# A hybrid block on one Trainium2 core: begun blocks stored from ScalarE's queue, and a fourth sum made on the way up

## The chip, the core and the metric

The kernel runs on one core of one Trainium2 chip. A core has five engines with instruction queues of their own: PE (TensorE, matrix products into the eight banks of PSUM), DVE (VectorE), ACT (ScalarE), POOL (GpSimd) and SP (SyncE, which here issues the transfers). Each engine takes its instructions in the order of its queue and waits on semaphores for the others. A transfer (DMA) is issued by an engine's queue and then runs on 16 DMA engines that all queues share. The metric is device time in microseconds (us), lower is better.

## What is computed

One layer over 1024 tokens of width 1024, in float32: three mixers side by side (mLSTM, stick-breaking attention, an S5 state space), an output projection, and then a gated feed-forward network (FFN). The change is in the FFN alone:

```python
h = rmsnorm(x, norm_ffn_g[l])
up = h @ ffn_w_up[l]                      # 1024 x (2 * 2816)
g, v = up[..., :D_FF], up[..., D_FF:]
g = causal_dwconv(g, ffn_conv_w[l])       # 3 taps along the tokens
x = x + (jax.nn.silu(g) * v) @ ffn_w_down[l]
```

## The kernel before

Values are split in two parts, high and low, and each product is made of three (high by high, high by low, low by high). Both matrix products of the FFN run by a Strassen-Winograd scheme: a 2 by 2 partition of the matrices with seven products instead of eight, in which sums of the quarters are multiplied.

On the way up, the 2816 hidden features are 22 blocks `f` of 128. `others` makes the sums of a block's weights on DVE (`ss`), and `split` casts each to its high part on ACT (`wh`) and subtracts for the low part on DVE (`wl`). `up` makes the products, twelve matmuls of 128x512 each (`product`), into banks `pw`, `pv` and `pz`: `b11`, `t2`, `b21`, `t1`, `t3`, `t4`, `b22`. DVE and ACT take them out: `u2 = pv + p1` and `u3` are partial sums, `tv` is the value half and `pad` (`gs` in the profile) the gate half, to which the convolution (`cv`, with a Silu on ACT) is applied, and `tv` becomes the gated result.

The products `b11` and `b21` need only the unsplit input's first half, so ten blocks (`NPRE`) are begun before the other sums are ready: `keep` makes these two products, `put` copies each from PSUM into a tile `p1` on ACT and stores it in device memory (`kept`). `up` of such a block loads them back, the first into a `p1` tile (`L646`, `p<-kept`), the second into the gate half (`L647`, `gs<-kept`). The `p1` tiles come from four buffers. `order` lets a begun block and one that wasn't begun follow each other; two such blocks are a pair.

At the end of each pair `up` makes the sums that the product on the way down needs from the two gated results `one` and `tv` (`L682` to `L687`): it stores `tv`, then `one` with its second half replaced by a difference, then `ts`. These are `bd[at, 0..2]`. On the way down `fetch` loads halves of them (`tr`), `tokens` splits them (`th`, `tl`), and for the operand `t4` it loads two and subtracts one from the other. Seven products over the eleven pairs follow.

The order of the instructions on each engine is set by the tile framework's scheduler from the order of the code, priorities and its own timeline; buffers of a pool are given out by tags. So the same lines may stand elsewhere in the queues when other lines are added. All transfers are on SP's queue.

Of the kernel before, what the change touches and what calls it, by code (L numbers as in the profile page):

```python
# [10 lines left out]
F32 = mybir.dt.float32  # L11
# [9 lines left out]
P = 128  # L21
# [13 lines left out]
HT = T // 2  # L35
# [45 lines left out]
class Kernel:  # L81
# [467 lines left out]
    def ffn(self):  # L549


        nc, a = self.nc, self.a
# [6 lines left out]
        NPAIR = NF // 2  # L559
        order = [f for x in zip(range(NPRE - 1), range(NPRE, 2 * NPRE - 1)) for f in x] + list(range(2 * NPRE - 1, NF)) + [NPRE - 1]  # L560
        bd = {(at, i): self.dram.tile([P, T], F32, name=f"bd{at}_{i}") for at in range(NPAIR) for i in range(3)}
        t1, t2 = slice(0, HT), slice(HT, T)

        def parts(x, tag):
# [28 lines left out]
        def product(ps, w, b, more=False):  # L593

            n = 0
            for k in range(4):
                (rh, rl), lh, ll = B[b][k], *(x[:, k * P:(k + 1) * P] for x in w)
                for l, r in ((lh, rh), (lh, rl), (ll, rh)):
                    nc.tensor.matmul(out=ps, lhsT=l, rhs=r, start=n == 0 and not more, stop=n == 11, skip_group_check=more)  # L599
                    n += 1  # L600


        kept = {f: self.dram.tile([2, P, HT], F32, name=f"kept{f}") for f in range(NPRE)}
# [9 lines left out]
        def put(f, i):  # L613
            pw = begun[f][0]
            s = half_tile("p1", 4)
            nc.scalar.copy(out=s, in_=pw)
            nc.sync.dma_start(out=kept[f][i - 1], in_=s)

        keep(0, 1)
        self.last_scale(bank("s"))  # L620
        st_fa, fa = self.pool("ffa", side="left", waits="tile")
        half_tile = lambda n, c: fa.tile([P, HT], F32, tag=n, name=n, bufs=c)
        put(0, 1)
        for f in range(NPRE):
            if f + 1 < NPRE:
                keep(f + 1, 1)
                put(f + 1, 1)
            keep(f, 2)
            put(f, 2)
# [11 lines left out]
        def up(f, w):  # L641
            pad = gs[f % 2]
            tv = fb.tile([P, T], F32, tag="tv", name="tv", bufs=3)
            p1, u2, u3 = half_tile("p1", 4), fb.tile([P, HT], F32, tag="u2", name="u2"), fb.tile([P, HT], F32, tag="u3", name="u3")
            if f in kept:
                nc.sync.dma_start(out=p1, in_=kept[f][0])  # L646
                nc.sync.dma_start(out=pad[:, 2:2 + HT], in_=kept[f][1])  # L647
            else:
                pw = bank("w")
                product(pw, w[1], "b11")  # L650
                nc.scalar.copy(out=p1, in_=pw)
            pv = bank("v")
            product(pv, w[6], "t2")
            self.add(u2, pv, p1)
            if f not in kept:
                product(pw, w[2], "b21", True)
                nc.scalar.copy(out=pad[:, 2:2 + HT], in_=pw)
            pz = bank("z")
            product(pz, w[5], "t1")
            pv = bank("v")  # L660
            product(pv, w[7], "t3")
            self.add(u3, pv, u2)
            self.add(tv[:, t2], pz, u3)
            pv = bank("v")
            product(pv, w[4], "t4")
            self.add(tv[:, t1], pv, u3)
            product(pz, w[3], "b22", True)
            self.add(pad[:, 2 + HT:2 + T], pz, u2)
            c = fb.tile([P, T], F32, tag="cv", name="cv", bufs=2)
            self.act(c, pad[:, 0:T], AF.Copy, scale=cw[:, f, 0:1])  # L670
            for i in range(1, 3):
                self.stt(c, pad[:, i:i + T], cw[:, f, i:i + 1], c, ALU.mult, ALU.add)
            self.act(c, c, AF.Silu)
            self.mul(tv, c, tv)
            at, second = divmod(order.index(f), 2)
            if not second:
                self.first = tv
                return

            one = self.first  # L680
            nc.sync.dma_start(out=bd[at, 0], in_=tv)
            ts = fb.tile([P, T], F32, tag="ts", name="ts")  # L682
            self.sub(ts[:, t1], tv[:, t2], one[:, t2])
            self.sub(one[:, t2], one[:, t2], one[:, t1])
            self.sub(ts[:, t2], tv[:, t2], one[:, t2])
            nc.sync.dma_start(out=bd[at, 1], in_=one)
            nc.sync.dma_start(out=bd[at, 2], in_=ts)  # L687

        def block(r, c, k):

            tag = ("wv", "wt")[k % 2]
            raw = wq.tile([P, 512], F32, tag=tag, name=tag, bufs=2)
            nc.sync.dma_start(out=raw, in_=a["w_dn"][order[2 * k + c]][:, r * 512:r * 512 + 512])
            return raw

        for f, after in zip(order, order[1:] + [None]):
            this = ws
            if after is not None:
                ws = others(after, *gate_row(after, after not in kept))
            else:  # L700
                early = [block(0, 0, k) for k in range(4)]
                early = [(raw, parts(raw, "wx")) for raw in early]
            up(f, this)
# [9 lines left out]
        operand = {"b21": (0, t1), "b22": (0, t2), "b11": (1, t1), "t1": (1, t2), "t3": (2, t1), "t2": (2, t2)}  # L713
# [3 lines left out]
        x = {}  # L717

        def fetch(n, k):
            at, cols = operand[n]  # L720
            r = dt.tile([P, HT], F32, tag="tr", name="tr", bufs=4)
            nc.sync.dma_start(out=r, in_=bd[k, at][:, cols])
            return r

        def tokens(n, k):
            r = fetch("b21" if n == "t4" else n, k)
            if n == "t4":
                self.sub(r, r, fetch("t2", k))
            w = tuple(dt.tile([P, HT], F32R, tag=t, name=t, bufs=6) for t in ("th", "tl"))
            self.split(w, r)  # L730
            return w
# [83 lines left out]
        for p, n in ((1, "b11"), (2, "b21"), (7, "t3"), (6, "t2"), (4, "t4"), (5, "t1"), (3, "b22")):  # L815
            chained, last = p in (2, 3), p == 3
            if not chained:
                ps = [bank("d") for _ in range(4)]
            ends = []
            for k in range(NPAIR):  # L820
                w, b = weights(p, k), tokens(n, k)
                if last and k >= NPAIR - 5:
                    ends.append((k, w, b))
                else:
                    for m in range(4):
                        accumulate(ps[m], k, m, w, b, chained)
                between(p, k)
            for m in range(4):
                for k, w, b in ends:
                    accumulate(ps[m], k, m, w, b, chained)  # L830
                for cols in (slice(0, 256), slice(256, 512)) if last and m == 3 else (t1,):
                    with self.tc.high_priority():
                        evict(p, m, ps[m][:, cols], cols)
# [819 lines left out]
```

## Time and profile before

| | us |
|---|---|
| median of 3 runs | 1221.27 (1219.47 to 1224.64) |
| the profiled execution's own time | 1223.04 |
| its span in the trace | 1221.3 |
| PE, DVE, ACT, POOL busy in the span | 1188.3, 968.1, 632.9, 107.2 |

The mean granted clock of TensorE is 0.997 of full speed. The span has four stretches here: all that lies ahead of the FFN, to 580.3 us; the begun blocks and the sums of the input, to 643.8; the way up, to some 1008.5; the way down, to 1217.5. Matmuls are pipelined, and a modelled duration of 0.39 us stands on each of 128x512, while they start 0.227 us apart. An engine's line in a timeline says when an instruction started, how long it took, and in brackets how long the engine had been idle and what the profile takes for the releaser.

### The profile page before, as it was taken

The numbers are of one execution on the slowest core, as the hardware profiler recorded it, in microseconds if no ns is written. First come the engines' busy times: TensorE is split into PE (matmuls) and PEld (weight loads), VectorE is DVE, ScalarE is ACT, GpSimd is POOL, SyncE is SP. The second block draws the span as 40 slices with busy tenths as digits, with TensorE's granted clock in tenths as the row PEclk, the third lists the DMA queues.
The fourth block names the chain that finished last, engine by engine and source line by source line (L and its number), as shares of the span: only waits on it lengthen the run. The fifth ranks groups of instructions, "written<-read, shape, count | busy, mean of one in ns | idle before, by whom it ended". The sixth has DMA issues, their size and how long they took to land.

```text
span 1221.3 us, 17857 instructions
## 1 busy us (share of the span) xinstructions
PE 1188.3 (97%) x6543; PEld 1020.1 (84%) x6543; DVE 968.1 (79%) x1645; ACT 632.9 (52%) x1106; POOL 107.2 (9%) x100
## 2 busy tenths in 40 slices
PE   7899999999999999999999999999999999999998
PEld 6898999988899897787778888888888887888787
DVE  7898988899876588757886888888888676787874
ACT  6433588878786634444653333333344346664441
POOL 0000110201004655100000000000000000000000
PEclk9999999999999999999999999999999999999999
DMA  6431420101104201375372434443333257884563
GB/s 230 145 64 43 104 70 1 35 18 54 42 27 115 61 8 53 110 232 167 124 253 80 133 134 138 137 127 107 121 121 97 94 176 258 267 276 145 161 206 115
DMA packets 78855, 148.15 MB, mean 121 GB/s; under 512 B 10376, under 2 KB 16144, under 8 KB 78768
## 3 DMA queue, kind: packets, MB, share of 16 engines
q1 hardware_dynamic: 78768, 147.02, 38.1%
q8 instruction: 51, 0.84, 0.3%
q14 instruction: 36, 0.29, 0.1%
HBM read 110.21 MB, written 36.18 MB: 120 GB/s over the span
## 4 chain that ended last, share of the span: by engine, by line
PE 65%; DVE 17%; issue 7%; DMA 6%; ACT 4%; SPq 1%; POOL 0%; DVEq 0%; POOLq 0%; ACTq 0%
PE pv L599 15%; PE pd L812 12%; PE pj L156 11%; PE pz L599 10%; PE pw L599 10%; DVE sl L1174 4%; DMA tr<-bd 2%; PE first L156 2%; DVE cacc L113 1%; DVE srl L97 1%; ACT sl L121 1%; DVE zn L97 1%; DMA qk<-qkd 1%; DVE srl L110 1%; ACT srl L121 1%
## 5 line engine op out<-in xcount | busy, mean ns | idle before, releaser
L516 ACT CAST wh<-ss 128x512 fp32r<-128x512 f32 x88 | 53.6, 618 | 128.1 <-PE pz L599 81.2
L812 PE MATMUL pd<-tl,wh 128*128 128x512 f32 x292 | 114.0, 390 | 2.0 <-DVE tl L97 2.0
L156 PE MATMUL pj<-wh,hh 128*128 128x256 f32 x384 | 111.5, 290 | 1.5 <-ACT sg L121 1.2
L812 PE MATMUL pd<-th,wh 128*128 128x512 f32 x292 | 111.3, 390 | 1.0 <-ACT th L516 1.0
L812 PE MATMUL pd<-th,wl 128*128 128x512 f32 x292 | 112.0, 389 | 0.0
L156 PE MATMUL pj<-wh,hl 128*128 128x256 f32 x384 | 109.7, 286 | 0.0
L156 PE MATMUL pj<-wl,hh 128*128 128x256 f32 x384 | 108.9, 284 | 0.0
L1174 DVE TENSOR_TENSOR_SCAN sl<-sl,srl 128x256 f32<-128x256 f32 (+3 forms) x90 | 75.5, 871 | 22.9 <-ACT sl L121 22.3
L156 PEld LDWEIGHTS pj<-wh,hh 128*128 128x128 f32 x384 | 73.3, 191 | 3.5 <-ACT sg L121 1.6
L156 PEld LDWEIGHTS pj<-wl,hh 128*128 128x128 f32 x384 | 73.3, 191 | 0.9 <-issue 0.2
L156 PEld LDWEIGHTS pj<-wh,hl 128*128 128x128 f32 x384 | 73.3, 191 | 0.4 <-issue 0.4
L516 ACT CAST th<-tr 128x512 fp32r<-128x512 f32 x77 | 47.3, 618 | 42.2 <-DVE tr L97 25.4
L121 ACT ACTIVATE sl<-sl 128x512 f32<-128x512 f32 x108 | 68.0, 630 | 1.4
L812 PEld LDWEIGHTS pd<-tl,wh 128*128 128x128 f32 x292 | 54.8, 188 | 14.5 <-DVE tl L97 3.1
L812 PEld LDWEIGHTS pd<-th,wh 128*128 128x128 f32 x292 | 54.7, 188 | 12.8 <-ACT th L516 1.4
L97 DVE TENSOR_TENSOR wl<-ss,wh 128x512 fp32r<-128x512 f32 x88 | 60.2, 686 | 5.7 <-ACT wh L516 4.5
L812 PEld LDWEIGHTS pd<-th,wl 128*128 128x128 f32 x292 | 54.8, 188 | 11.2
L97 POOL TENSOR_TENSOR wl<-wr,wh 128x512 fp32r<-128x512 f32 x28 | 38.3, 1368 | 286.3 <-DVE wh L142 203.2
L113 DVE SCALAR_TENSOR_TENSOR cv<-gs,prm,cv 128x1024 f32<-128x1024 f32 x44 | 56.4, 1281 | 3.9 <-ACT cv L121 3.8
L97 DVE TENSOR_TENSOR tl<-tr,th 128x512 fp32r<-128x512 f32 x77 | 52.3, 685 | 7.4 <-ACT th L516 7.4
L1200 PEld LDWEIGHTS pv<-sbv,saT 128*128 128x128 f32 x432 | 53.9, 192 | 1.8
L1200 PE MATMUL pv<-sbv,saT 128*128 128x64 f32 x432 | 53.4, 269 | 0.0
(480 smaller groups left out, 3414.1 us busy)
## 6 DMA issues: line engine op xcount, KB each, us to landing
tr<-bd SPq DMA_DIRECT2D x88, 256.0 KB, 3.3
wt<-w_up SPq DMA_DIRECT2D x44, 256.0 KB, 2.7
bd<-tv SPq DMA_DIRECT2D x22, 512.0 KB, 2.9
wv<-w_up SPq DMA_DIRECT2D x32, 256.0 KB, 3.0
wr<-w_up SPq DMA_DIRECT2D x32, 256.0 KB, 3.2
wv<-w_dn SPq DMA_DIRECT2D x30, 256.0 KB, 3.5
wr<-w_out SPq DMA_DIRECT2D x28, 256.0 KB, 3.3
wt<-w_dn SPq DMA_DIRECT2D x25, 256.0 KB, 4.0
```

The lines of the kernel that those rows point to most:

```text
L97: (eng or self.nc.vector).tensor_tensor(out=out, in0=a, in1=b, op=op)
L110: (eng or self.nc.vector).tensor_scalar(out=out, in0=a, scalar1=s1, scalar2=s2, op0=op0, **kw)
L113: self.nc.vector.scalar_tensor_tensor(out=out, in0=a, scalar=s, in1=b, op0=op0, op1=op1)
L121: self.nc.scalar.activation(out=out, in_=a, func=f, **kw)
L156: self.nc.tensor.matmul(out=ps, lhsT=l, rhs=r, start=n == 0, stop=n == last)
L516: self.nc.scalar.copy(out=hi, in_=x)
L599: nc.tensor.matmul(out=ps, lhsT=l, rhs=r, start=n == 0 and not more, stop=n == 11, skip_group_check=more)
L812: nc.tensor.matmul(out=ps, lhsT=l, rhs=r, start=k == 0 and n == 0 and not chained, stop=k == NPAIR - 1 and n == 2, skip_group_check=chained)
L1174: nc.vector.tensor_tensor_scan(out=l[:, s], data0=l[:, s], data1=rl[:, s], initial=0.0 if b == 0 else self.sb_last, op0=ALU.add, op1=ALU.add)
L1200: nc.tensor.matmul(out=out[:, i, :], lhsT=aT[:, (at + q) * P:(at + q + 1) * P], rhs=self.sbv[i - b - q][:, h * SBD:(h + 1) * SBD], start=b ...
```

## The change

The begun blocks' stores are issued on ACT's queue in place of SP's. And the fourth sum, `tv[:, t1] - ts[:, t2]`, is made at the end of each pair into a `p1` tile and stored (`bd4`, 256 KB), so that `tokens` loads it as it loads the others.

```diff
+        bd4 = [self.dram.tile([P, HT], F32, name=f"bd{at}_4") for at in range(NPAIR)]
...
             s = half_tile("p1", 4)
             nc.scalar.copy(out=s, in_=pw)
-            nc.sync.dma_start(out=kept[f][i - 1], in_=s)
+            nc.scalar.dma_start(out=kept[f][i - 1], in_=s)
...
             nc.sync.dma_start(out=bd[at, 1], in_=one)
             nc.sync.dma_start(out=bd[at, 2], in_=ts)
+            t4 = half_tile("p1", 4)
+            self.sub(t4, tv[:, t1], ts[:, t2])
+            nc.sync.dma_start(out=bd4[at], in_=t4)
...
         def fetch(n, k):
-            at, cols = operand[n]
             r = dt.tile([P, HT], F32, tag="tr", name="tr", bufs=4)
-            nc.sync.dma_start(out=r, in_=bd[k, at][:, cols])
+            if n == "t4":
+                nc.sync.dma_start(out=r, in_=bd4[k])
+            else:
+                at, cols = operand[n]
+                nc.sync.dma_start(out=r, in_=bd[k, at][:, cols])
             return r

         def tokens(n, k):
-            r = fetch("b21" if n == "t4" else n, k)
-            if n == "t4":
-                self.sub(r, r, fetch("t2", k))
+            r = fetch(n, k)
```

The scheduler sets the order of much of the way up anew. Two places follow, both at the end of the fourth pair (blocks 3 and 13; the next begun block is 4). The first is SP's queue. `bd_0`, `bd_1` and `bd_2` are the pair's three stores, `gs<-kept` and `p<-kept` the loads of the two kept products. `kept_6451` is block 5. Before:

```order
L647 DMA gs_7007<-kept_6451 128x512
L572 DMA wt<-w_up 128x512
L681 DMA bd_0_6422<-tv 128x1024
L646 DMA p_8414<-kept_6451 128x512
L686 DMA bd_1_6423<-tv 128x1024
L572 DMA wt<-w_up 128x512
L572 DMA wr<-w_up 128x512
L687 DMA bd_2_6424<-ts 128x1024
```

The same place of the changed kernel, where `kept_6462` is block 5, `kept_6461` block 4, and `bd_4` the new store:

```order
L648 DMA gs_7018<-kept_6462 128x512
L573 DMA wv<-w_up 128x512
L682 DMA bd_0_6422<-tv 128x1024
L687 DMA bd_1_6423<-tv 128x1024
L688 DMA bd_2_6424<-ts 128x1024
L647 DMA p_8165<-kept_6461 128x512
L691 DMA bd_4_6449<-p_8118 128x512
L573 DMA wt<-w_up 128x512 x2
```

The load into `p` has moved from behind the pair's first store to behind its third, and it is now that of block 4, which comes next, where before it was that of block 5, one pair further on.

The second place is DVE's queue there. `u_8143` and `u_8144` are block 4's `u2` and `u3`, `p_8142` its loaded `p1`, `wl` the low parts of weights. Before:

```order
L97 TENSOR_TENSOR u_8143<-pv,p_8142 128x512
L97 TENSOR_TENSOR wy<-wv,wx 128x512
L113 SCALAR_TENSOR_TENSOR cv<-gs_7007,prm,cv 128x1024
L97 TENSOR_TENSOR wl<-ss,wh 128x512
L113 SCALAR_TENSOR_TENSOR cv<-gs_7007,prm,cv 128x1024
L97 TENSOR_TENSOR u_8144<-pv,u_8143 128x512
L97 TENSOR_TENSOR wl<-wt,wh 128x512
L97 TENSOR_TENSOR tv<-pz,u_8144 128x512
L97 TENSOR_TENSOR tv<-cv,tv 128x1024
L97 TENSOR_TENSOR tv<-pv,u_8144 128x512
L97 TENSOR_TENSOR wl<-ss,wh 128x512
L97 TENSOR_TENSOR ts<-tv 128x512
```

In the changed kernel, where block 4's are `p_8165`, `u_8166` and `u_8167`, and `p_8118` is the new sum of the pair:

```order
L97 TENSOR_TENSOR tv<-cv,tv 128x1024
L97 TENSOR_TENSOR ts<-tv 128x512
L97 TENSOR_TENSOR wl<-ss,wh 128x512
L97 TENSOR_TENSOR tv<-tv 128x512
L97 TENSOR_TENSOR ts<-tv 128x512
L97 TENSOR_TENSOR p_8118<-tv,ts 128x512
L97 TENSOR_TENSOR u_8166<-pv,p_8165 128x512
L97 TENSOR_TENSOR u_8167<-pv,u_8166 128x512
L97 TENSOR_TENSOR tv<-pz,u_8167 128x512
L97 TENSOR_TENSOR tv<-pv,u_8167 128x512
L97 TENSOR_TENSOR wl<-wt,wh 128x512
```

Block 4's partial sums, made ahead of the last pair's gating and sums before, now stand behind them and behind the new sum.

## Rows read from the trace of the kernel before

**Rows 1.** Busy us (instructions) of PE, PEld, DVE, ACT, POOL, clock, DMA by stretch
```profile
580.30:643.80 63.50, 61.41 (x263) 48.41 (x262) 53.25 (x88) 38.74 (x70) 0.00 (x0) 1.00 0.59 191
643.80:1008.50 364.70, 364.70 (x1610) 302.08 (x1610) 297.36 (x416) 139.76 (x205) 0.00 (x0) 1.00 0.38 122
1008.50:1217.50 209.00, 206.00 (x904) 169.05 (x903) 150.31 (x241) 104.38 (x186) 0.00 (x0) 1.00 0.63 206
...
757.28:789.92 32.64, 32.64 (x146) 27.04 (x145) 27.89 (x41) 12.34 (x19) 0.00 (x0) 1.00 0.39 133
```

**Rows 2.** Timeline of PE (start us, us, instruction, [idle before, releaser]), begun blocks
```profile
613.35 0.39 PE L599 MATMUL pw<-b11h,wy 128*128 128x512 f32 x1
614.26 0.50 PE L599 MATMUL pw<-b11h,wx 128*128 128x512 f32 x1 [0.53 <-ACT wx L516]
614.60 0.40 PE L599 MATMUL pw<-b11l,wx 128*128 128x512 f32 x1
...
620.55 0.50 PE L599 MATMUL pw<-b11h,wx 128*128 128x512 f32 x1 [0.53 <-ACT wx L516]
```

**Rows 3.** Timeline of ACT, begun blocks
```profile
613.59 0.62 ACT L516 CAST wx<-wr 128x512 fp32r<-128x512 f32 x1 [0.38 <-ACT t4h L516]
```

**Rows 4.** Waits of SP's queue, 570 to 660 us: us in total, times, longest
```profile
SPq L617 <- ACT p L616: 25.4, 10, 4.9
```

**Rows 5.** Instructions on the tile `kept`: ns least, median, most, first and last start
```profile
L617 SPq DMA_DIRECT2D kept<-p x20: 319/326/391, 590.5 to 643.5; - x20
```

**Rows 6.** The chain of waits in order of time (start us, us), way up
```profile
696.59 8.16 PE pv L599 x36
```

**Rows 7.** Timeline of DVE, one pair on the way up
```profile
773.92 0.69 DVE L97 TENSOR_TENSOR gs<-pz,u 128x512 f32<-128x512 f32 x1 [1.79 <-PE pz L599]
...
775.13 0.69 DVE L97 TENSOR_TENSOR u<-pv,p 128x512 f32<-128x512 f32 x1
...
778.71 1.28 DVE L113 SCALAR_TENSOR_TENSOR cv<-gs,prm,cv 128x1024 f32<-128x1024 f32 x1
779.90 0.68 DVE L97 TENSOR_TENSOR u<-pv,u 128x512 f32<-128x512 f32 x1
...
784.04 0.68 DVE L97 TENSOR_TENSOR ts<-tv 128x512 f32<-128x512 f32 x1
784.64 0.69 DVE L97 TENSOR_TENSOR ss<-wt 128x512 f32<-128x512 f32 x1
...
787.05 0.68 DVE L97 TENSOR_TENSOR ts<-tv 128x512 f32<-128x512 f32 x1
```

**Rows 8.** Timeline of SP's queue at the end of the pair before that
```profile
750.54 0.33 SPq L681 DMA_DIRECT2D bd<-tv  x1
750.92 0.42 SPq L646 DMA_DIRECT2D p<-kept  x1
```

**Rows 9.** Transfers issued from 660 to 1000 us: KB each, median us to landing
```profile
bd<-tv SPq DMA_DIRECT2D x20, 512.0 KB, 2.9
wt<-w_up SPq DMA_DIRECT2D x37, 256.0 KB, 2.7
bd<-ts SPq DMA_DIRECT2D x10, 512.0 KB, 4.2
```

**Rows 10.** The ten loads of line 646, `p<-kept`, of the whole span
```profile
DMA to landing us min/median/max: 2.9/3.4/5.3
```

**Rows 11.** Busy us by microsecond, columns as in rows 1, ahead of the FFN
```profile
42.00:43.00 1.00, 0.00 (x0) 0.00 (x0) 0.12 (x2) 0.99 (x4) 0.00 (x0) 1.00 0.45 172
...
44.00:45.00 1.00, 0.00 (x0) 0.00 (x0) 1.00 (x6) 1.00 (x3) 0.00 (x0) 1.00 0.03 8
...
46.00:47.00 1.00, 1.00 (x6) 1.00 (x6) 0.14 (x1) 0.00 (x0) 0.00 (x0) 0.77 0.98 332
...
49.00:50.00 1.00, 1.00 (x4) 1.00 (x4) 1.00 (x4) 0.00 (x0) 0.87 (x1) 0.52 0.13 25
```

**Rows 12.** Timeline of PE on the way down, operand `t4`
```profile
1146.18 0.50 PE L812 MATMUL pd<-tl,wh 128*128 128x512 f32 x1 [1.80 <-DVE tl L97]
1146.51 0.39 PE L812 MATMUL pd<-th,wl 128*128 128x512 f32 x1
```

## The prediction

> **What bounds the kernel now.** I read a table of the busy times by stage first, since the page's 97% for TensorE (PE) is a mean over stages [rows 1]. In the gated stage on the way up, 643.8 to 1008.5 us, PE is busy for all of its 364.70 us. One pair of blocks takes 32.64 us there, all of it PE: 144 products of 128x512 at 8.16 us for 36 [rows 6]. Nothing can be gained in this stage; whatever makes PE wait in it is added to the time. In the same 32.64 us VectorE (DVE) works 27.89 us, so it has 4.75 us to spare for each pair. PE waits 2.1 us while blocks are begun (580.3 to 643.8) and 3.0 us from 1008.5 on [rows 1]. The chain of waits, the lines of single engines and the landing times of the transfers then price what the change moves.
>
> **Part 1, the begun blocks' stores go to ScalarE (ACT).** SP loses 20 issues, and with them the waits for ACT's copies, 25.4 us in all [rows 4], in which the `w_up` loads queued behind stood still. What is that worth? PE's gaps here look like a wait for the cast of a weight that was loaded late. The rows say otherwise: the product before the gap starts its last matmul at 613.35 and, at 8.16/36 = 0.227 us each, is done with it at 613.58; the cast starts at 613.59 and takes 0.62; PE resumes at 614.26 [rows 2, 3]. The cast waits for its buffer, which that product was reading, not for the load. There are five such gaps, the last at 620.55 [rows 2]. So an earlier load gives 0, and I take 0. ACT gains 20 issues; one on SP takes 0.32 to 0.39 us [rows 5], so 6.4 to 7.8 us more in a stretch in which ACT works 38.74 of 63.50 [rows 1]. Its idle time covers them; without that cover, all on the path, it is +7.8. Bounds 0 to +7.8.
>
> The Trainium skill (DMA: Bandwidth & Descriptors, Queues, rings and completion order) says that each DMA engine takes turns between the queues that have work for it, so ACT's stores would now run among SP's loads instead of ahead of or behind them. No row of before has two busy queues. By the rule a load beside a store lands later by at most the store's own share, which the same cover hides; the sum stays, and the upper bound is the likelier end.
>
> **Part 2, on the way down.** Eleven loads and eleven subtractions go, with all that DVE waited for them. But PE pays only what shows on PE, 1.80 us at 1146.18, where the matmul behind the wait takes 0.50 for 0.39 [rows 12]. I take -2.0, bounds -3.0 (all PE idle after 1008.5, [rows 1]) to 0.
>
> **Part 3, on the way up.** For each pair DVE gains one subtraction, 0.60 us from start to start [rows 7], and SP one 256 KB store. 0.60 of 4.75 spare costs nothing by itself. What costs is where the load of the next pair's first partial result (`p<-kept`) now stands. The sum's tile is taken from the same four `p1` buffers, and in the order of the changed kernel that load has moved behind the third store of the pair, on SP, while the addition that reads it is now the instruction directly behind the new sum on DVE. Before, the load is issued at 750.92, right behind a pair's first store [rows 8], and the addition that reads it runs at 775.13 [rows 7]: 24 us of cover. Now there is none: DVE, and everything queued behind that addition, stands until the load lands.
>
> Who waits for that? There are eight PSUM banks. When PE comes to the second block's `t4` product, the pair's first block holds four banks (t2, t1 with b22, t3, t4) and the second block four (pw, t2, t1, t3). The bank for `t4` is the one that this addition frees. This closes a loop, and I add it up once round, from the second block's `t4` product to the same product a pair later:
> (a) PE, from `t4` through the second block's `b22`: by its order 12 of `t4`, 8 of the next block's t2, 12 of the first block's b22, the other 4 of t2, 36 of the next block's t1, t3 and t4, 8 of b11 and 12 of b22 = 92 matmuls x 0.2267 = 20.9 us [rows 6].
> (b) DVE from the eviction into `gs` to the end of the last `ts`. The same stretch before takes 787.05 + 0.68 - 773.92 = 13.8 us [rows 7]. In the changed order it has fifteen instructions, twelve of 512 columns at 0.60 and three of 1024 at 1.20 = 10.8 [rows 7], 10.9 with the last one's tail. I take 12.0: the evictions are gone from it, but the two waits for ACT's `cv` stay. Bounds 10.9 and 13.8.
> (c) SP issues the store of `ts` and then the load: 0.4 [rows 8].
> (d) The load lands. Median 3.4, between 2.9 and 5.3 [rows 10]; a store that stands behind others, as `bd<-ts` does, takes 4.2 where the first one, `bd<-tv`, takes 2.9 [rows 9]. This load stands behind two such stores: I take 3.9, bounds 2.9 and 5.3.
> (e) The addition itself, 0.7 [rows 7].
> (f) Ahead of `gs` DVE's order now holds an addition that waits for a `wt` load; that load stands on SP behind a split of DVE's own. It lands in 2.7 [rows 9]; between 0 and all of that comes on top. I take half, 1.4.
> Sum: 20.9 + 12.0 + 0.4 + 3.9 + 0.7 + 1.4 = 39.3 us, bounds 35.8 and 44.8. The pair's PE work is 32.64, so PE stands 6.7 us in each pair (3.2 to 12.2).
>
> The Trainium skill (DMA: Bandwidth & Descriptors, Rules for kernel authors) tells to issue a DMA early and wait late, which this change undoes; its fit for one DMA, 2.0 us and bytes over 436e3, would make (d) an estimate of 2.6 us and the whole 9 us less. No landing of this load in the trace is that short.
>
> How often? The load of the first pair's successor has cover: there PE still has those 92 matmuls, 20.9 us, against 12.0 + 0.8 + 3.9 + 0.7 = 17.4. Seven loads follow in the same position (blocks 2 to 8). 7 x 6.7 = 47 us, bounds 22 and 85.
>
> **The clock.** PE was nearly idle between 42 and 45 us of the trace; in the microsecond from 46 its granted clock fell from 1.00, 2.4 GHz, to a mean of 0.77, and in the one to 50 it was still 0.52, 1.2 GHz [rows 11]. That is half of some 3.2 us lost, 1.6. A pair's 6.7 us of standing comes in two pieces (a smaller one at `b21`, whose bank waits for a copy on ACT that stands behind the same chain). So 0 to 2 x 1.6 per pair; I take 1.0: +7, bounds 0 and 22.
>
> **Sum** against the profiled execution's 1223.04 us: 0 - 2.0 + 47 + 7 = +52, so 1275. The median of the runs, 1221.27, is 1.8 lower: **1273 us**.
>
> **The rivals.**
> *The loop as summed, with PE standing in every pair from the third on*: 1273 with its own bounds from 22 - 3 to some 85. For it: DVE and SP take their instructions in order. Chance 0.67 that it comes out between 1246 and 1292.
> *The clock falls at both pieces of every pair, and the weights behind the late loads come late too*: (f) at 2.7 and the clock at 22 give 7 x 8.0 + 22 - 2 = +76, 1297. For it: [rows 11]; against: the pieces are shorter than the idle stretch there. Chance 0.17.
> *The loop at its low ends*: 7 x 3.2 - 2 = +20, 1242. For it: few transfers run beside the load. Chance 0.10.
> *The cover holds*: it decides from a loop of 32.64, for which (b) to (f) would have to stay under 11.7 us; even (b) with (e) at their least are 11.6, so the load would have to be in before the sums. Then only -2.0 is left: 1219. Chance 0.04.
> *Faster*: the up stage stays full, and the gaps outside of it close: the 2.1 us of begun blocks (if the casts do wait for loads after all, at the point where the SP queue no longer holds them) and the 3.0 on the way down [rows 1], with the slow first matmul after each gap, 0.1 for each [rows 2]: -5 to -6.5, 1215. It is the other side. Against it: the 0.01 us between the product's end and the cast [rows 2, 3]. Chance 0.02.
> That the stores don't leave SP, or that the sum stays on the way down, the order rules out.
>
> **How the numbers follow.** The likeliest is 1273. The range leaves out the cover, the faster case and about half of each outer one: 1244 to 1300. 0.5% is 6.1 us, about what a measurement of this kernel can tell from no change. Slower by more than that: 0.67 + 0.17 + 0.10 = 0.94; within: 0.04; faster: 0.02.
>
> **What would show it.** In the changed kernel's table by stage, the stretch from 643.8 us on should last some 405 to 430 us for what took 364.7, with PE standing twice in each pair, DVE idle some 3 us ahead of the addition `u<-pv,p`, put down to the DMA of `p`, and a period of about 39 to 40 us. The landing of that load should be near 3.9. The five gaps at the begun blocks should still be there, and the one of 1.80 us on the way down gone. I am wrong if the period is 32.64, or if PE stands for anything but that addition and the ACT copy behind it; the granted clock tells the size of the last term.

## The result, and the profile after

The changed kernel takes **1286.39 us**, the median of 5 runs (1284.20 to 1290.42), beside 1222.13 for the kernel before on the same chip (1219.47 to 1224.64). The ratio is 1.0521, with a 95% interval of 1.0503 to 1.0540. That is 64 us more, on the side that was predicted, and 13 us above the predicted 1273.

The profiled execution spans 1284.9 us, 63.6 more than before. Its page and its table by stage (busy us of PE, PEld, DVE, ACT, POOL, granted clock, DMA share) say where they went:

```profile
PE 1211.7 (94%) x6543; PEld 1032.5 (80%) x6543; DVE 971.7 (76%) x1645; ACT 633.1 (49%) x1106; POOL 107.3 (8%) x100
...
580.30:643.80 63.50, 61.54 (x264) 48.42 (x263) 53.25 (x88) 38.82 (x70) 0.00 (x0) 1.00 0.61 194
643.80:1072.50 428.70, 388.45 (x1612) 314.49 (x1611) 306.23 (x426) 137.68 (x203) 0.00 (x0) 0.95 0.32 108
1072.50:1285.00 212.50, 206.24 (x899) 169.31 (x897) 145.37 (x231) 106.55 (x189) 0.00 (x0) 0.99 0.60 195
```

The begun blocks are as they were [rows 1]. The way up takes 428.70 us for what took 364.70. PE is idle for 40.3 of them, and its busy time in the whole span has grown by 23.4, from 1188.3 to 1211.7, with the same number of matmuls, since they ran at a granted clock of 0.95 on the way up. Stands (stretches in which PE waits) and slower matmuls together make up the 63.6 us.

What PE and DVE waited for on the way up (us in total, times, longest), and the landing of line 647, the load `p<-kept`:

```profile
PE pv L600 <- DVE u L97: 29.5, 7, 5.1
PE pw L600 <- ACT p L652: 10.4, 8, 2.3
PE pz L600 <- DVE tv L97: 0.4, 1, 0.4
...
DVE u L97 <- DMA p<-kept: 28.1, 8, 3.9
```
```profile
DMA to landing us min/median/max: 4.0/4.1/4.7
```

One pair's end on DVE's and SP's lines, where before there were the rows of [rows 7] and [rows 8]:

```profile
800.77 0.68 DVE L97 TENSOR_TENSOR gs<-pz,u 128x512 f32<-128x512 f32 x1
...
812.06 0.69 DVE L97 TENSOR_TENSOR ts<-tv 128x512 f32<-128x512 f32 x1
812.79 0.69 DVE L97 TENSOR_TENSOR p<-tv,ts 128x512 f32<-128x512 f32 x1
817.25 0.69 DVE L97 TENSOR_TENSOR u<-pv,p 128x512 f32<-128x512 f32 x1 [3.77 <-DMA p<-kept]
```
```profile
812.78 0.32 SPq L688 DMA_DIRECT2D bd<-ts  x1
813.15 0.54 SPq L647 DMA_DIRECT2D p<-kept  x1
813.79 1.13 SPq L691 DMA_DIRECT2D bd<-p  x1
```

The load is issued at 813.15, lands some 4.1 later, and the addition runs at 817.25: nothing is left of the 24 us of cover before. PE's lines at the two places where it stands, with the restart before that, and the table of the same stretch:

```profile
776.83 0.51 PE L600 MATMUL pv<-t4h,wh 128*128 128x512 f32 x1 [4.75 <-DVE u L97]
...
778.42 0.63 PE L600 MATMUL pv<-t4l,wh 128*128 128x512 f32 x1
778.84 0.63 PE L600 MATMUL pv<-t4h,wl 128*128 128x512 f32 x1
...
809.88 0.50 PE L600 MATMUL pw<-b21h,wx 128*128 128x512 f32 x1 [1.22 <-ACT p L652]
...
817.99 0.68 PE L600 MATMUL pv<-t4h,wh 128*128 128x512 f32 x1 [5.09 <-DVE u L97]
```
```profile
772.00:776.80 4.80, 0.08 (x1) 0.00 (x0) 0.95 (x2) 0.00 (x0) 0.00 (x0) 1.00 0.85 296
776.80:779.00 2.20, 2.17 (x6) 1.75 (x7) 1.98 (x3) 0.00 (x0) 0.00 (x0) 0.59 0.00 0
779.00:781.00 2.00, 2.00 (x7) 1.57 (x6) 0.00 (x0) 0.00 (x0) 0.00 (x0) 0.60 0.00 0
781.00:784.00 3.00, 3.00 (x14) 2.44 (x14) 0.69 (x1) 0.62 (x1) 0.00 (x0) 1.00 0.16 20
```

From one `t4` product to the same a pair later, 776.83 to 817.99, are 41.16 us; over the six pairs from 736.31 to 982.80 the mean is 41.08, for 32.64 us of PE work. After the stand the matmuls start 0.42 to 0.43 us apart until 780.55, where at 2.4 GHz they start 0.23 apart: the clock is at its lower level, 1.2 GHz (0.59 and 0.60 are means of stretches that hold some of both). From 779.00 to 781.00 nothing runs beside PE, no transfer and no other engine, so the slow spacing there is no contention.

### The profile page after: what moved, and what is told of

It is laid out like the page before. It is cut to its first block, busy times and chain, and to the rows that moved or that the text cites. A ratio compares the mean times of both kernels' runs of the same rounds, so it can differ in the third digit from the quotient of the medians.

```text
span 1284.9 us, 17888 instructions
## 1 busy us (share of the span) xinstructions
PE 1211.7 (94%) x6543; PEld 1032.5 (80%) x6543; DVE 971.7 (76%) x1645; ACT 633.1 (49%) x1106; POOL 107.3 (8%) x100
## 4 chain that ended last, share of the span: by engine, by line
PE 52%; DVE 23%; DMA 10%; issue 7%; ACT 6%; SPq 1%; POOL 0%; DVEq 0%; ACTq 0%; POOLq 0%
PE pd L817 15%; PE pj L156 11%; PE pv L600 9%; PE pw L600 6%; PE pz L600 5%; DVE sl L1179 3%; DMA wt<-w_up 2%; DMA p<-kept 2%; DVE wl L97 2%; DVE ss L97 2%; DVE cacc L113 1%; DVE tv L97 1%; DVE srl L97 1%; DMA wr<-w_up 1%; ACT sl L121 1%
## 5 line engine op out<-in xcount | busy, mean ns | idle before, releaser
L516 ACT CAST wh<-wt 128x512 fp32r<-128x512 f32 x40 | 24.8, 621 | 105.6 <-PE pv L600 93.6
L600 PE MATMUL pv<-t4h,wh 128*128 128x512 f32 x88 | 41.0, 466 | 29.5 <-DVE u L97 29.5
```

Of the source, the lines that this page charges most:

```text
L516: self.nc.scalar.copy(out=hi, in_=x)
```

## Experiments

All ratios are against the kernel before on the same chip. Two hypotheses stood at the start. Mine: the tile taken from the `p1` ring (its four buffers, given out in turn) moves the next begun block's load behind the pair's stores and its addition behind the pair's gating, and PE stands for that. The rival: the change's own work (DVE's subtraction, SP's 256 KB store, ACT's twenty issues) is what costs.

**The two parts apart.** First the queue of the stores alone:

```diff
-            nc.sync.dma_start(out=kept[f][i - 1], in_=s)
+            nc.scalar.dma_start(out=kept[f][i - 1], in_=s)
```

> The kernel before with one edit: the begun blocks' twenty stores are issued on ACT's queue. PE's and DVE's orders are those of before, word for word. My theory (part 1 of the prediction): PE's five gaps there are casts that wait for PE itself to finish with their buffer, so nothing changes: 1222 us, between 1219 and 1225, and five gaps of about 0.5 us remain. Rival one: the loads that stood behind the stores' waits were what the casts waited for, the gaps close: 1218 to 1219. Rival two: ACT's twenty issues at 0.32 to 0.39 us push its casts back: up to 1229. Rival three: half of the loss of the changed kernel comes from here: over 1240.

Measured: 1221.72 us, ratio 0.9999 (0.9989 to 1.0009). This part is worth nothing that can be told from the noise. The waits of PE from 580 us on, in the kernel before and in this one:

```profile
PE pw L599 <- ACT wx L516: 2.1, 4, 0.5
```
```profile
PE pw L599 <- ACT wx L516: 1.9, 4, 0.5
```

PE waits as before for the casts, four times. Some transfers of the begun stage do feel it: the stores of `kept` land in a median of 3.5 us on ACT's queue for 2.4 on SP's, the loads into `wv` in 4.2 for 3.2, those into `wr` in 3.4 as before. PE's idle time there doesn't grow.

Then the changed kernel with that line undone, so the fourth sum alone:

> The changed kernel with the begun blocks' stores back on SP's queue, so the fourth sum alone. PE's and DVE's orders are those of the changed kernel, word for word. My theory: the whole loss comes from the sum's part, 1286 us, between 1282 and 1291, with seven stands of PE ahead of t4 of 3.6 to 5.1 us each. Rival: the two parts act together (ACT's queue busy with stores while loads come late), and the time is below 1270.

Measured: 1284.79 us, ratio 1.0509 (1.0489 to 1.0530), with seven stands ahead of `t4` and a mean period of 40.81 us. The whole loss belongs to the sum's part.

**The sum without the ring.** The changed kernel with one word of place:

```diff
-            t4 = half_tile("p1", 4)
+            t4 = c[:, t1]
             self.sub(t4, tv[:, t1], ts[:, t2])
```

> The changed kernel with one edit: the fourth sum is made in the first half of the block's cv tile, whose value is dead by then, and not in a tile of the p1 ring. Sum, store and the loads on the way down stay. In the order built from it the load of the next begun block's first product stands again right behind the pair's first store, as in the kernel before, and the addition that reads it stands ahead of the last pair's gating. My theory (the ring's turn put the load late, and nothing else costs): PE is full again on the way up, period 32.64 us, and only the way down differs: 1219 to 1223 us. Rival one: DVE's eleven more subtractions or SP's eleven more stores of 256 KB are on the path (0.6 us and 2.6 us a pair): 1229 to 1250. Rival two: the sum's place in the ring is innocent: 1286.

Measured: 1218.98 us, ratio 0.9976 (0.9966 to 0.9986). The same subtractions and the same stores cost nothing here. The way up in its table by stage, the load on SP's queue, its landing, and all that PE waits for from 580 us on:

```profile
643.80:1008.50 364.70, 364.70 (x1611) 301.98 (x1610) 303.22 (x426) 139.41 (x205) 0.00 (x0) 1.00 0.39 129
```
```profile
748.57 0.33 SPq L682 DMA_DIRECT2D bd<-tv  x1
748.95 0.42 SPq L647 DMA_DIRECT2D p<-kept  x1
751.58 0.32 SPq L687 DMA_DIRECT2D bd<-tv  x1
```
```profile
DMA to landing us min/median/max: 2.8/3.4/5.2
```
```profile
PE pw L600 <- ACT wx L516: 1.9, 4, 0.5
PE pd L817 <- ACT th L516: 0.6, 1, 0.6
```

The load stands again behind the pair's first store, nobody waits for it, and PE is busy in every microsecond of the way up. DVE works 303.22 us in the stretch for 297.36 before [rows 1]: ten more subtractions that the spare time takes in. PE's idle time on the way down has shrunk from 3.0 us [rows 1] to 0.6, and from its first to its last matmul that stretch takes 212.8 us for 216.0. This version is faster than both kernels, though than the one before by only 3 us (0.24%), which its interval just tells from no change. To see whether the stores' queue has a share in that, the same with the stores on SP:

> The version with the sum in the cv tile, with the begun blocks' stores back on SP's queue: the fourth sum alone, made without the ring. My theory: the 3 us gained come from PE's stands on the way down (3.0 us before, 0.6 in the version with both), and the queue of the stores is worth nothing: 1219 us, within 1 us of that version. Rival: the gain, or part of it, came from the queue: 1221 to 1222.

Measured: 1218.98 us, ratio 0.9976 (0.9966 to 0.9985). The queue has none.

**The ring without the sum.** The kernel before, with a tile taken from the ring for next to nothing:

```diff
+        bd4 = [self.dram.tile([P, 1], F32, name=f"bd{at}_4") for at in range(NPAIR)]
...
+            t4 = half_tile("p1", 4)
+            nc.vector.tensor_copy(out=t4[:, 0:1], in_=ts[:, T - 1:T])
+            nc.sync.dma_start(out=bd4[at], in_=t4[:, 0:1])
```

> The kernel before with one edit: at the end of each pair a tile is taken from the p1 ring, one column of ts is copied into it, and that column (512 bytes in all) is stored. No fourth sum, no 256 KB store, the way down and the queue of the begun blocks' stores as before. In the order built from it the load of the next begun block's first product stands behind the pair's last store, as in the changed kernel. My theory (the late load alone makes the loss): the loop of the changed kernel less some 0.5 us for the shorter instruction on DVE, so a period of 39.5 to 41 us and 1275 to 1288 us. Rival: the sum and its store make the loss, and a tile of the ring costs nothing: 1222 to 1228.

Measured: 1334.00 us, ratio 1.0920 (1.0898 to 1.0942), well outside what either hypothesis said. The transfers issued on the way up (KB each, median us to landing) and DVE's wait:

```profile
p<-kept SPq DMA_DIRECT2D x10, 256.0 KB, 8.6
...
bd<-p SPq DMA_DIRECT2D x10, 0.5 KB, 8.9
```
```profile
DVE u L97 <- DMA p<-kept: 72.9, 8, 11.6
```

The store of 512 bytes, 4 on each of 128 partitions, takes 8.9 us to land, and the load, which here stands behind it on SP's queue, 8.6. (In the changed kernel the new store stands behind the load.) The loop follows: its period is 46.07 us, 5.0 above the changed kernel's, for a landing that is 4.5 later. So the small store went:

> The ring's tile once more, without the small store that stood ahead of the late load in the run before (there the load took 8.6 us to land, and the store of 512 bytes 8.9). The kernel before with one edit: at the end of each pair a tile is taken from the p1 ring and one column of ts is copied into it; nothing is stored. The load of the next begun block's first product stands directly behind the pair's last store. My theory (the late load alone makes the loss, and the run before was longer by what its load landed later): landing 3.3 to 4.2 us, a period of 40 to 41.5 us, and 1275 to 1288 us. Rival one: without the sum and its store the loss is gone: 1222 to 1228. Rival two: the tile of the ring itself costs what the run before showed: above 1310.

Measured: 1287.78 us, ratio 1.0537 (1.0522 to 1.0553), landing in 3.9, period 40.60. Without the sum and without any new store the loss is that of the changed kernel. A tile of the ring alone, with a copy of one column into it, makes it. No run gives the ring a fifth buffer, so whether that would bring the load forward again stays open.

**The landing out of the loop.** The changed kernel, the late load on another queue:

```diff
-                nc.sync.dma_start(out=p1, in_=kept[f][0])
+                nc.gpsimd.dma_start(out=p1, in_=kept[f][0])
```

> The changed kernel with one edit: the begun blocks' first products are loaded by POOL's queue, which has nothing else to do in the FFN. The sum stays in the p1 ring, and on DVE the addition that reads the load stays directly behind it; the load itself waits now for nothing but its buffer, which an earlier pair's sum has left a pair before, so that it lands long ahead. My theory in two parts: the landing (4.1 us) goes out of the loop, and what is left of it, 20.9 of PE, 1.0 of the wait for a weight, 11.5 of DVE up to the last ts, 0.7 for the new sum and 0.7 for the addition, is 34.8 us, still over 32.64: PE stands some 2 us a pair, 1225 to 1245 us, most likely 1236. Rival one: the landing was all: PE full, 1218 to 1223. Rival two: the load's place was innocent: 1280 or more.

Measured: 1244.60 us, ratio 1.0188 (1.0171 to 1.0205), at the upper end of what I expected. No instruction waits for the load now. One of these loads, an addition on DVE's line, and PE's waits from 580 us on:

```profile
804.54 0.54 POOL L647 DMA_DIRECT2D p<-kept  x1 [35.23 <-DMA bd<-p]
```
```profile
824.23 0.68 DVE L97 TENSOR_TENSOR gs<-pz,u 128x512 f32<-128x512 f32 x1
...
836.29 0.69 DVE L97 TENSOR_TENSOR p<-tv,ts 128x512 f32<-128x512 f32 x1
836.90 0.68 DVE L97 TENSOR_TENSOR u<-pv,p 128x512 f32<-128x512 f32 x1
```
```profile
PE pw L600 <- ACT p L652: 9.8, 8, 2.0
PE pv L600 <- DVE u L97: 4.3, 5, 1.2
PE pd L817 <- ACT th L516: 2.5, 1, 2.5
PE pw L600 <- ACT wx L516: 1.9, 4, 0.5
PE pd L817 <- ACT wh L516: 1.8, 1, 1.8
```

The load issued at 804.54 is the one that the addition at 836.90 reads; it landed in 2.9 us, 29 us ahead, so its buffer had been free that long. The addition follows the sum at once, yet the same `t4` product comes every 35.07 us (730.62 to 941.05, six pairs), 2.4 over PE's work. The expected 34.8 are met. The load's place is one part of the loss, 1286.39 - 1244.60 = 41.8 us. The rest is 1244.60 - 1218.98 = 25.6. I put it down to the addition's place on DVE behind gating and sums, by the sum that gave 34.8; no run moves the addition alone. Of these 25.6 the way down has 5.7 (218.5 us from its first to its last matmul for 212.8), with two stands of 1.8 and 2.5 us.

**The clock.** Twenty more matmuls behind each `b21` of the blocks that aren't begun, where PE would stand:

```diff
                 product(pw, w[2], "b21", True)
+                for k in range(20):
+                    nc.tensor.matmul(out=pw, lhsT=w[2][0][:, 0:P], rhs=B["b21"][0][0], start=False, stop=True, skip_group_check=True)
```

> The changed kernel with one edit: behind each b21 product on the way up (the twelve blocks that aren't begun) 20 more matmuls of 128x512 are added onto its bank, 4.5 us of PE work each time, just ahead of the t4 product where PE stands; the gate half of these blocks is another number by that. It is for the clock. The order built from it takes b22 some 18 matmuls earlier, so the loop shrinks by 4.1 us while PE's work in a pair grows to 37.2. My theory: the spacing of 0.43 us after each stand comes from PE having stood. Filled, PE hardly stands, all matmuls are 0.227 apart, the granted clock stays at 1.00, the period is 37.2 to 38.5 us and the time 1222 + 12 x 4.5 = 1276, up to 1286: not longer than the changed kernel, for 54 us more of PE work. Rival: the slow spacing comes from what runs beside it at that place (transfers, DVE and ACT reading banks): it stays, some 3 us in each pair, 1295 to 1305.

Measured: 1284.85 us, ratio 1.0517 (1.0501 to 1.0532), with pairs of 38.5 us. PE does 12 x 20 x 0.227 = 54 us more, and the kernel isn't longer than the changed one. Its way up, PE's waits from 580 us on, and a row of DVE's line:

```profile
643.80:1070.00 426.20, 419.84 (x1845) 345.61 (x1844) 303.60 (x428) 139.00 (x205) 0.00 (x0) 1.00 0.33 109
```
```profile
PE pw L600 <- ACT p L652: 6.4, 6, 1.3
PE pd L819 <- ACT th L516: 2.5, 1, 2.5
PE pw L600 <- ACT wx L516: 1.9, 4, 0.5
```
```profile
817.65 0.69 DVE L97 TENSOR_TENSOR u<-pv,p 128x512 f32<-128x512 f32 x1 [4.54 <-DMA p<-kept]
```

The load is late as in the changed kernel (DVE waits for it eight times, 20.3 us in all for 28.1 there; the last row is the longest wait), but PE has work, the granted clock stays at 1.00, and no row of slow matmuls follows on the way up. The slow spacing came from the stands: this run shows it, and the changed kernel's own row from 779.00 to 781.00, with nothing beside PE, rules the rival out there. What this run doesn't part is how much of the shorter period is the clock's and how much the earlier `b22`'s.

## Why the prediction was right, and where it was off

**Part 1, 0:** measured 0, and [rows 2, 3] were the right ones to ask. The gaps are four, not five. The upper bound, which I had called the likelier end, didn't show. The Trainium skill (DMA: Bandwidth & Descriptors, Queues, rings and completion order) has the DMA engines take turns between queues; the trace of `queue_alone` fits that, with 1.0 us more for the `wv` loads and 1.1 for the stores, though the `wr` loads land no later. The cover hid it.

**Part 2, -2.0:** right in kind, hidden in the changed kernel. In `sum_in_cv` it is worth -3.0 us, the lower bound. In the changed kernel the 1.80 us stand is gone as said, but the way down begins with a new one:

```profile
1079.44 0.50 PE L817 MATMUL pd<-th,wh 128*128 128x512 f32 x1 [1.79 <-ACT wh L516]
```

The gating of the last blocks, which ends later, stands ahead of that cast on ACT (an activation at 1076.15, the cast at 1078.78), and 2.8 us are lost to slower matmuls behind the stand. From its first to its last matmul the way down takes 216.8 us for 216.0. I had taken its start as untouched; that was a miss of some 3 us.

**Part 3, the loop:** the mechanism was right in each link: seven stands at `t4` for DVE's addition, eight smaller ones at `b21` for ACT's copy behind the same chain. Its terms, as means over the six pairs from 736.31 to 982.80:

| term | predicted | measured |
|---|---|---|
| (a) PE from `t4` through `b22` | 20.9 | 23.4 |
| (b) DVE from `gs` to the last `ts` | 12.0 | 11.4 |
| (c) + (d) issue and landing of the load | 0.4 + 3.9 | 4.5 |
| (e) the addition | 0.7 | 0.75 |
| (f) the wait for a weight ahead of `gs` | 1.4 | 0.95 |
| period | 39.3 | 41.08 |

The landing is 4.1: the store that stands behind other stores, 4.2 [rows 9], was nearer to it than the load's own median of before, 3.4 [rows 10], and 3.9 lay between them. The Trainium skill's fit for one DMA (DMA: Bandwidth & Descriptors, Anatomy of one DMA — SWDGE (gpsimd) path), stated there for transfers that GpSimd issues, gives an estimate of 2.6 us. On SP's queue behind the pair's stores the trace disagrees, 4.1; for the same load issued by POOL, that is GpSimd, `load_on_pool` with a median of 2.9 nearly agrees. Terms (b) and (f) were half a microsecond too long each, so the stands came to 40.3 us where the sum had 47. The loop's upper bound was added up wrong: its terms make 43.8, not 44.8, so 11.2 us of standing in a pair and 78 in all, not 12.2 and 85; likeliest value and range don't hang on it.

**The clock, +7:** this is the step that failed in size. PE's busy time grew by 23.4 us, over three times the term and just above its upper bound of 22. I took 1.0 us a pair, less than the 1.6 of the one fall in [rows 11]. But a fall follows the stand at `t4` in every pair, and it costs 1.7 us in the first three (from 777.56 on there are seven spacings of 0.42 to 0.43 in a row) and 2.6 to 2.9 in the last four (from 983.40 on there are twelve). That makes 16 us. The smaller stand at `b21` cost another 1.3 and 1.6 where it was 2.3 and 2.0 us long, and only a slow first start, 0.1, where it was 1.0 to 1.2. The new stand on the way down, which I hadn't in the sum, cost 2.8. The matmuls behind `t4` lie in term (a), on the loop, and are 2.2 of the 2.5 us by which (a) is longer; the rest is that in two of the six pairs it holds 96 matmuls and not 92.

So the sum read 0 - 2.0 + 47 + 7 = 52, and the runs gave about 0 + 0 + 40 + 23 = 63. Two errors of opposite sign, 7 us too much for the stands and 16 too little for the clock, and the -2.0 that didn't show left the time 13 us above the forecast and inside the range; that the two partly cancel is luck. The rival with the clock falling and (f) at 2.7, 1297, came near the clock's size, 22 us, by two falls of 1.6 in each pair where the trace has mostly one that costs more, and had (f) wrong. **The cover holds** fell with its own condition. Its price was wrong as well: in `load_on_pool` the load is in before the sums, as that rival asks, and the time is 1244.60 and not 1219, since (a), (b), (e) and the new sum alone (20.9 + 11.4 + 0.75 + 0.7 = 33.8) are over 32.64.

## What to carry to other kernels

In this kernel a tile taken from a pool's tag was also a turn in that tag's order: the load that took the next turn was scheduled behind it, though its buffer had long been free. So look at who else draws from the tag before borrowing from it, and prefer a tile that is dead at that point. Where two results meet on one in-order engine, add up the loop through that engine and the buffers that it frees, and compare it with the busy engine's work: what is over stands in every round. Then price each stand twice, for itself and for the matmuls after it; here the second, 23.4 us, was more than half of the first, 40.3.

## What the runs showed of the hardware

- A store of 4 bytes from each of 128 partitions, ahead of the load on SP's queue, took 8.9 us to land, and the 256 KB load behind it 8.6. Without that store the load landed in 3.9. The changed kernel's 256 KB store, which stands behind the load, took 4.2.
- After a stand of 4.75 us the granted clock was 0.59 and 0.60 in the next two stretches of some 2 us, with matmuls 0.43 us apart (1.2 GHz) until 3.7 us after the restart, also while no transfer and no other engine was busy. Other stands of 3.6 to 5.1 us were followed by up to 2.9 us lost in this way. Where PE had 20 more matmuls to do at that place, the clock stayed at 1.00, and 54 us of added work made the kernel no longer.
- With the begun blocks' stores on ACT's queue they landed in 3.2 to 3.6 us (medians of five kernels) for 2.4 to 2.5 on SP's, the loads into `wv` beside them in 3.5 to 4.2 for 3.0 to 3.4, and those into `wr` no later. `queue_alone` shows that it cost no time.
